# A feed-forward's first product by Strassen's algorithm, seven sub-products for eight

## The chip, the cores and the metric

The kernel runs on one core of a Trainium2 chip, in one launch. The metric is the device time of the whole program in microseconds; where several runs are compared, it is their median. The engines are TensorE (PE in the profile; its weight loads stand apart as PEld), VectorE (DVE), ScalarE (ACT), GpSimd (POOL) and SyncE (SP), which issues the DMAs. Each takes its instructions in the order in which they were queued, and they wait for each other by semaphores.

## The reference

The program is one inference step of a trunk of two layers over 640 tokens: 512 latent tokens and 128 context tokens, each of 1024 features. A layer is a feed-forward, a group of mixers and a second feed-forward, each on a normalised and modulated input and each added back through a gate:

```
x += gate1 * 0.5 * SwiGLU_1(mod(norm(x)))
x += gate2 * W_out [MLA | SWA-GQA+sink | bi-GatedDeltaNet](mod(norm(x)))
x += gate3 * 0.5 * SwiGLU_2(mod(norm(x)))

def swiglu(h, w1, w2):
    gate, up = jnp.split(h @ w1, 2, axis=-1)
    return (jax.nn.silu(gate) * up) @ w2
```

The inner width of a feed-forward is 2816, so `w1` is 1024 x 5632 and `w2` is 2816 x 1024. The shifts, scales and gates come from `silu(cond) @ w_ada + b_ada` (adaLN), with one condition for the latent tokens and one for the context tokens. All of it is in float32. The change touches the four feed-forwards, the adaLN work that is done inside them, and the end of each stage.

## The kernel before, in words

Activations are kept transposed: features on the 128 partitions, the 640 tokens along the row, in 8 tiles `x[0]` to `x[7]`. For precision every factor of a large product is split in two float32r parts, `hi` (a rounded copy, made by ScalarE) and `lo` (the rest, source minus `hi`, made by VectorE): `split`, which calls L67 and L70. A product is then three matmuls, hi x hi, lo x hi and hi x lo. `weight` loads a weight tile by a DMA on SP's queue and splits it in pieces of 128x512; `linear` (L104) runs the products of one 128-column weight block with all 640 tokens in two halves of 320 columns (`HALVES`), each in a PSUM bank of its own. A weight block of the first product is 8 feature tiles x 3 x 2 halves, 48 matmuls.

A feed-forward (`ffn`) starts with `modnorm`, which scales, shifts and splits the input (L169 to L171). Then it works in two halves of the inner width. In each half it goes over 11 column blocks `j`: the gate's 128 columns, SiLU on ScalarE (L229), the up-projection's 128 columns, the multiplication on VectorE (L232), and the split of the result in a pair of `mid` tiles. After the 11 blocks come the 8 output tiles `n` of the second product, each with 11 x 3 x 2 matmuls and an addition to `x` through the gate (`residual`, `addgate`, L188). The statistics of the next normalisation (`rstd`, `spread`) are computed at the last output tile.

The adaLN values that are needed later are computed in between: `fill` inserts one whole job of `adaln` behind a column block or an output tile. A job loads 8 tiles of 128x512 and multiplies each by the two conditions and accumulates (the first tile on ScalarE, L267; 7 x 2 steps on VectorE, L269), splits the two sums (ScalarE, and GpSimd at L273), sums over the partitions with 4 small matmuls (L275) and transposes the result with 4 more (L280).

The instructions are put on the engines' queues by a planner before the run: it follows the order of the program where it can, takes a later instruction when the earlier ones of that engine aren't ready by its own cost model, and lets an instruction wait for a buffer of its tag. `bufs` gives how many buffers a tag has: 3 for raw weight tiles, 4 for `whi` and for `wlo`, 22 for `mid`, 6 PSUM banks for products.

Two other lines serve in what follows as examples of operations beside each other: the rotary embedding in the mixer (`rope`, L307 and L309 on GpSimd, L308 on VectorE) and the convolution there (L395).

Of the kernel before, what the change touches and what calls it, by code (L numbers as in the profile page):

```python
# [6 lines left out]
F32 = mybir.dt.float32  # L7
# [14 lines left out]
NJ = DFF // P  # L22
EPS = 1e-6
# [18 lines left out]
class Net:  # L42
# [26 lines left out]
    def lo(self, dst, src, hi):  # L69
        self.nc.vector.tensor_tensor(dst, src, hi.bitcast(F32), ALU.subtract)  # L70

# [5 lines left out]
    def split(self, src, hi, lo):  # L77
        self.hi(hi, src)
        self.lo(lo, src, hi)

    def weight(self, src, kt, m):
        raw = self.wraw.tile([P, kt, m], F32, tag="wraw", name=self.nm("wr"))
        self.nc.sync.dma_start(raw, src)
        step = 512 // m
        out = []
        for k in range(0, kt, step):
            n = min(step, kt - k)
            hi, lo = (self.wsp.tile([P, n, m], F32R, tag=t, name=self.nm(t)) for t in ("whi", "wlo"))
            self.split(raw[:, k:k + n], hi, lo)
            out += [(hi[:, i, :], lo[:, i, :]) for i in range(n)]  # L90
        return out
# [35 lines left out]
    def rstd(self, pool, kind="G", windows=(0, 128, 256, 384, 512), last=True):  # L127

        nc = self.nc
        nb = len(windows)  # L130
        ps = self.pt(kind)
        r0, r = (pool.tile([P, nb], F32, tag="rs", name=self.nm("rs"), bufs=2) for _ in range(2))
        for i, t in enumerate(self.sq):
            for b, c in enumerate(windows):
                self.lastmm = nc.tensor.matmul(ps[:, 2 * b:2 * b + 2], lhsT=t[:, c:c + P], rhs=self.ones[:, :2],
                                               start=(i == 0 and b == 0), stop=(i == 1 and b == nb - 1))
# [56 lines left out]
    def residual(self, k, w, rhs, G, squares):  # L193


        if not squares:
            return self.addgate(k, self.linear(w, rhs), G)
        sq = self.xp.tile([P, T], F32, tag="sq", name=self.nm("sq"), bufs=3)
        if k < KD - 1:
            i = self.addgate(k, self.linear(w, rhs), G, sq)  # L200
            self.addsquare(sq)
            return i
        self.addsquare(sq)
        pool = _Bufs(self.const, dict(rs=4))
        ps = self.linear(w, rhs, cols=HALVES[:1])
        self.addgate(k, ps, G, sq, 0)
# [4 lines left out]
        ps += self.linear(w, rhs, cols=HALVES[1:], after={(5, 0): m, (10, 0): self.lastmm})  # L211
        i = self.addgate(k, ps, G, sq, 1)
        self.r = [row, self.rstd(pool, "G", WINDOWS[1])]
        return i


    def ffn(self, w1, w2, A, B, G):
        nc = self.nc
        with self.pool("ffn") as fp, self.banks(L=6, G=2):
            self.adap = fp  # L220
            h = self.modnorm_in(fp, A, B)
            for half in range(2):
                js = range(half * NJ // 2, (half + 1) * NJ // 2)
                mid = []
                for j in js:
                    pg = self.linear(self.weight(w1[j], KD, P), h)
                    sg = fp.tile([P, T], F32, tag="sg", name=self.nm("sg"), bufs=2)
                    for p, (c0, cw) in zip(pg, HALVES):
                        i1 = nc.scalar.activation(sg[:, c0:c0 + cw], p[:, :cw], AF.Silu)  # L229
                    pu = self.linear(self.weight(w1[NJ + j], KD, P), h)  # L230
                    for p, (c0, cw) in zip(pu, HALVES):
                        i0 = nc.vector.tensor_tensor(sg[:, c0:c0 + cw], p[:, :cw], sg[:, c0:c0 + cw], ALU.mult)  # L232
                    hi = fp.tile([P, T], F32R, tag="mid", name=self.nm("mh"), bufs=22)
                    lo = fp.tile([P, T], F32R, tag="mid", name=self.nm("ml"), bufs=22)
                    self.split(sg, hi, lo)
                    mid.append((hi, lo))
                    if j - js[0] in (3,5,7,9):
                        self.fill(i0, i1)
                for n in range(KD):
                    i0 = self.residual(n, self.weight(w2[half, n, :, :8], 8, P) + self.weight(w2[half, n, :, 8:], 3, P), mid, G, half == 1)  # L240
                    if n in (0,2,4):
                        self.fill(i0, i1)
# [5 lines left out]
    def adaln(self, l, i, start=False):  # L248
# [4 lines left out]
        ps = self.pt("G")  # L253
        if start:
            for q in range(KD):
# [3 lines left out]
        else:  # L259
            acc = [ap.tile([P, 512], F32, tag=t, name=self.nm(t), bufs=2) for t in ("ada0", "ada1")]  # L260
            for q in range(KD):
                raw = ap.tile([P, 512], F32, tag="adaw", name=self.nm("adaw"), bufs=4)
                nc.sync.dma_start(raw, a['wada'][l, i, q])
                for g in range(2):
# [3 lines left out]
                    else:  # L268
                        nc.vector.scalar_tensor_tensor(acc[g], raw, c, acc[g], ALU.mult, ALU.add)  # L269
            for g in range(2):  # L270
                hi, lo = (ap.tile([P, 512], F32R, tag=t, name=self.nm(t), bufs=1) for t in ("adah", "adal"))
                self.hi(hi, acc[g])
                nc.gpsimd.tensor_tensor(lo, acc[g], hi.bitcast(F32), ALU.subtract)  # L273
                for n, x in enumerate((hi, lo)):
                    nc.tensor.matmul(ps[:2, :], lhsT=self.sel[:, g, :], rhs=x, start=(g + n == 0), stop=(g + n == 2))  # L275
        row = ap.tile([2, 512], F32, tag="adarow", name=self.nm("adarow"), bufs=1)
# [16 lines left out]
    def fill(self, *after):  # L293

        if len(self.jobs) > self.hold:
            with self.tc.issue_after(after[0].ins), self.tc.issue_after(after[1].ins):
                self.adaln(*self.jobs.pop(0))
# [17 lines left out]
    def mixer(self, l, A, B, G):  # L315
# [180 lines left out]
        with self.pool("wo") as wp:  # L496
# [19 lines left out]
            with self.banks(L=6, G=2):  # L516
                order = (8, 9, 10, 11, 4, 5, 6, 7, 0, 1, 2, 3)
                for n in range(KD):
                    w = self.weight(a['wo'][l, n, :, 8:], 4, P) + self.weight(a['wo'][l, n, :, :8], 8, P)
                    w = w[:4] + w[8:] + w[4:8]  # L520
                    self.residual(n, w, [o[i] for i in order], G, True)
# [540 lines left out]
    def body(self):  # L1062
# [6 lines left out]
        self.wraw, self.wsp = E("wraw", 3), E("wsp", 4)  # L1069
# [28 lines left out]
        self.jobs = []  # L1098
        with self.pool("ada") as self.adap, self.banks(G=2, N=1):
            for i in (0, 2, 1, 3):  # L1100
                self.adaln(0, i, start=True)
# [32 lines left out]
        self.jobs, self.hold = [(0, i) for i in range(4, 18)], 0  # L1134
        for l in range(L):
            self.hold = 0
# [3 lines left out]
            if l + 1 < L:  # L1140
                self.jobs = [(l + 1, i) for i in range(18)]
                self.hold = 11
            self.ffn(a['w1b'][l], a['w2b'][l], *mods(2))
        with self.pool("fin") as fp, self.banks(G=4):
# [65 lines left out]
def _layout(x):  # L1210
# [9 lines left out]
    for s, n in (('a', 'ffn1'), ('b', 'ffn2')):  # L1220
        out['w1' + s] = tiles(x[n + '_w1'], KD, P)
        out['w2' + s] = C(x[n + '_w2'].reshape(L, 2, NJ // 2, P, KD, P).transpose(0, 1, 4, 3, 2, 5))
# [51 lines left out]
```

## Time and profile before

| | us |
|---|---|
| median of 3 runs | 3321.58 |
| lowest and highest | 3320.39, 3327.34 |
| the profiled execution's own time | 3325.07 |
| span of the profile, first to last instruction | 3323.3 |

The profile shows one execution. Busy times are sums over instructions, as shares of the span; TensorE's matmuls are pipelined, so that the duration of one is longer than the distance from one to the next. A group of rows is named by source line, engine, operation and tiles, "out<-in". The mean granted clock of TensorE is 0.987 of its full rate.

### The profile page before, as it was taken

The numbers are of one execution on the slowest core, as the hardware profiler recorded it, in microseconds if no ns is written. First come the engines' busy times: TensorE is split into PE (matmuls) and PEld (weight loads), VectorE is DVE, ScalarE is ACT, GpSimd is POOL, SyncE is SP. The second block draws the span as 40 slices with busy tenths as digits, with TensorE's granted clock in tenths as the row PEclk, the third lists the DMA queues.
The fourth block names the chain that finished last, engine by engine and source line by source line (L and its number), as shares of the span: only waits on it lengthen the run. The fifth ranks groups of instructions, "written<-read, shape, count | busy, mean of one in ns | idle before, by whom it ended". The sixth has DMA issues, their size and how long they took to land.

```text
span 3323.3 us, 56733 instructions
## 1 busy us (share of the span) xinstructions
PE 3241.5 (98%) x22036; PEld 3129.5 (94%) x22036; DVE 1886.3 (57%) x4357; ACT 1384.8 (42%) x3041; POOL 452.2 (14%) x480
## 2 busy tenths in 40 slices
PE   8999999999998999999999999999999989999998
PEld 5999999999887999999999999999998879999998
DVE  4564577686885355643346735477878653433333
ACT  3332334554676433322233323255466763321222
POOL 0000011222343100100000100012114340000000
PEclk9999999999999999999999999999999999999999
DMA  6443453322714224522224534333235242222222
GB/s 212 128 149 116 134 164 127 97 76 91 201 54 138 84 86 133 155 94 72 69 92 143 156 99 139 98 103 110 72 121 152 75 138 74 69 73 74 83 65 76
DMA packets 180190, 364.78 MB, mean 110 GB/s; under 512 B 28112, under 2 KB 68176, under 8 KB 179920
## 3 DMA queue, kind: packets, MB, share of 16 engines
q1 hardware_dynamic: 179920, 361.15, 35.2%
q8 instruction: 173, 2.83, 0.4%
q14 instruction: 97, 0.79, 0.1%
HBM read 315.03 MB, written 46.04 MB: 109 GB/s over the span
## 4 chain that ended last, share of the span: by engine, by line
PE 87%; DVE 6%; ACT 3%; DMA 2%; issue 2%; SPq 0%; POOL 0%; POOLq 0%; DVEq 0%; ACTq 0%
PE psL L104 72%; PE psT L942 3%; PE psG L703 3%; PE psS L1036 2%; PE psT L931 1%; PE psG L275 1%; PE psS L742 1%; DMA of<-do 1%; PE psS L745 1%; ACT pr L910 1%; PE psS L981 1%; DVE hf L169 1%; DMA adaw<-in_wada_dram 0%; DVE wlo L70 0%; PE psS L776 0%
## 5 line engine op out<-in xcount | busy, mean ns | idle before, releaser
L70 DVE TENSOR_TENSOR wlo<-wr,whi 128x512 fp32r<-128x512 f32 (+2 forms) x726 | 494.2, 682 | 709.5 <-ACT whi L67 708.0
L67 ACT ACTIVATE whi<-wr 128x512 fp32r<-128x512 f32 (+2 forms) x726 | 446.2, 616 | 876.2 <-PE psL L104 614.9
L104 PE MATMUL psL<-hb,whi 128*128 128x320 f32 x1968 | 523.8, 313 | 0.7 <-DVE hb L171 0.5
L104 PE MATMUL psL<-hc,whi 128*128 128x320 f32 x1952 | 521.0, 314 | 0.0
L104 PE MATMUL psL<-ha,whi 128*128 128x320 f32 x1856 | 492.3, 312 | 5.0 <-DVE ha L171 3.7
L104 PE MATMUL psL<-hd,whi 128*128 128x320 f32 (+1 forms) x1856 | 486.3, 310 | 1.9 <-DVE hd L171 1.9
L104 PE MATMUL psL<-mh,wlo 128*128 128x320 f32 x1408 | 434.2, 309 | 0.0
L104 PE MATMUL psL<-ml,whi 128*128 128x320 f32 x1408 | 434.0, 309 | 0.0
L104 PE MATMUL psL<-mh,whi 128*128 128x320 f32 x1408 | 432.9, 310 | 0.0
L104 PEld LDWEIGHTS psL<-hb,whi 128*128 128x128 f32 x1968 | 351.9, 189 | 2.6 <-DVE hb L171 1.2
L104 PEld LDWEIGHTS psL<-hc,whi 128*128 128x128 f32 x1952 | 349.4, 189 | 0.8
L104 PEld LDWEIGHTS psL<-ha,whi 128*128 128x128 f32 x1856 | 329.8, 188 | 8.6 <-DVE ha L171 5.7
L104 PEld LDWEIGHTS psL<-hd,whi 128*128 128x128 f32 (+1 forms) x1856 | 328.9, 188 | 5.2 <-DVE hd L171 3.1
L269 DVE SCALAR_TENSOR_TENSOR ada<-adaw,cs,ada 128x512 f32<-128x512 f32 x448 | 313.7, 743 | 0.0
L104 PE MATMUL psL<-hb,wlo 128*128 128x320 f32 (+1 forms) x984 | 307.3, 312 | 0.0
L104 PE MATMUL psL<-hc,wlo 128*128 128x320 f32 (+1 forms) x976 | 305.6, 313 | 0.0
L104 PE MATMUL psL<-hd,wlo 128*128 128x320 f32 (+1 forms) x928 | 287.7, 310 | 0.0
L104 PE MATMUL psL<-ha,wlo 128*128 128x320 f32 (+1 forms) x928 | 287.5, 311 | 0.0
L104 PEld LDWEIGHTS psL<-ml,whi 128*128 128x128 f32 x1408 | 264.0, 188 | 2.8
L104 PEld LDWEIGHTS psL<-mh,whi 128*128 128x128 f32 x1408 | 263.5, 188 | 3.0
L104 PEld LDWEIGHTS psL<-mh,wlo 128*128 128x128 f32 x1408 | 264.1, 188 | 2.0
L273 POOL TENSOR_TENSOR adal<-ada,adah 128x512 fp32r<-128x512 f32 x64 | 89.8, 1404 | 1041.7 <-ACT adah L67 823.3
(299 smaller groups left out, 5612.1 us busy)
## 6 DMA issues: line engine op xcount, KB each, us to landing
adaw<-in_wada_dram SPq DMA_DIRECT2D x288, 256.0 KB, 2.9
wr<-in_w1a_dram SPq DMA_DIRECT2D x88, 512.0 KB, 3.7
wr<-in_w1b_dram SPq DMA_DIRECT2D x88, 512.0 KB, 3.5
wr<-in_win_dram SPq DMA_DIRECT2D x54, 512.0 KB, 3.5
wr<-in_w2a_dram SPq DMA_DIRECT2D x32, 512.0 KB, 4.0
wr<-in_w2b_dram SPq DMA_DIRECT2D x32, 512.0 KB, 3.5
wr<-in_wo_dram SPq DMA_DIRECT2D x16, 512.0 KB, 3.6
dqn<-hd SPq DMA_DIRECT2D x24, 320.0 KB, 3.1
```

What stands on the lines that cost most here:

```text
L67: self.nc.scalar.activation(dst, src, AF.Copy)
L70: self.nc.vector.tensor_tensor(dst, src, hi.bitcast(F32), ALU.subtract)
L104: i = nc.tensor.matmul(p[:m, :cw], lhsT=w[:, :m], rhs=r[:, c0:c0 + cw], start=(k == 0 and n == 0), stop=(k == kt - 1 and n == 2))
L169: nc.vector.scalar_tensor_tensor(t[:, c0:c0 + n], self.x[k][:, s], A[:, k, g:g + 1], r[j][:, c0:c0 + n], ALU.mult, ALU.mult)
L269: nc.vector.scalar_tensor_tensor(acc[g], raw, c, acc[g], ALU.mult, ALU.add)
L273: nc.gpsimd.tensor_tensor(lo, acc[g], hi.bitcast(F32), ALU.subtract)
L275: nc.tensor.matmul(ps[:2, :], lhsT=self.sel[:, g, :], rhs=x, start=(g + n == 0), stop=(g + n == 2))
L703: nc.tensor.matmul(p[:, s], lhsT=lhs[:, s], rhs=rhs[:, s], start=True, stop=True)
L742: nc.tensor.matmul(p1[:, :P], lhsT=qw[:, u, c, 64 * d:64 * d + P], rhs=S, start=True, stop=True)
L745: nc.tensor.matmul(p2[:, :P], lhsT=KD_[d][c][:, us], rhs=UU[d][:, us], start=True, stop=True)
L942: nc.tensor.matmul(po[:, oc:oc + w], lhsT=vv[:, vb, :], rhs=hl[ti][:, s0:s0 + w], start=(n == 0), stop=(n == len(place) - 1))
L1036: nc.tensor.matmul(p[:, j, :w], lhsT=x[:96, qc], rhs=y[:96, k0 + j * w:k0 + j * w + w], start=(i == 0), stop=(i == 2))
```

## The change

The gate's and the up-projection's column block `j` are taken together as a 256-row by 1024 matrix in 2 x 2 parts, `a11` and `a12` for the gate's first and second 512 features, `a21` and `a22` for the up-projection's. The input is taken in 2 x 2 parts too, by feature halves and by column halves of 320 tokens. From the third block on, `block` computes the product by Strassen's algorithm in Winograd's form: four sums of weights `s1` to `s4` on GpSimd for each block, four sums of activations `t1` to `t4` once for each feed-forward (`sums` in `combos`, on GpSimd, split by ScalarE and VectorE), seven products of 4 feature tiles x 3 matmuls, and additions of the results out of PSUM on VectorE. Two of the seven `lo` parts (`a12`, `a22`) are made by GpSimd. The first two blocks are multiplied as before. `combos` takes the place of `modnorm` in the feed-forwards; GpSimd adds the shift to the unsplit input, which the sums need, and these unsplit tiles lie in the `mid` buffers, of which there are 12.

The inner width is worked in four passes of 5, 5, 6 and 6 blocks, each followed by its share of the second product, so that an output tile is added to `x` four times. The adaLN jobs become generators, cut in five portions; `fill` runs two behind each block and one behind every second output tile. Twelve jobs are done in the first feed-forward, ten in the second, ten in the third, none in the fourth (14, 7, 11 and 0 before). Raw weight tiles are loaded in pieces of 128x512, with 6 buffers. The last two output tiles of a feed-forward are closed together (`closing`): first halves of both, the statistics, then the second halves.

```diff
+PASSES = (5, 5, 6, 6)
...
-    def split(self, src, hi, lo):
+    def split(self, src, hi, lo, gpsimd=False):
         self.hi(hi, src)
-        self.lo(lo, src, hi)
+        (self.nc.gpsimd if gpsimd else self.nc.vector).tensor_tensor(lo, src, hi.bitcast(F32), ALU.subtract)
...
+    def parts(self, raw, gpsimd=False):
+
+        hi, lo = (self.wsp.tile([P, *raw.shape[1:]], F32R, tag=t, name=self.nm(t)) for t in ("whi", "wlo"))
+        self.split(raw, hi, lo, gpsimd)
+        return [(hi[:, i, :], lo[:, i, :]) for i in range(raw.shape[1])]
...
     def weight(self, src, kt, m):
...
         step = 512 // m
...
+        return [w for k in range(0, kt, step) for w in self.parts(self.load(src[:, k:min(k + step, kt)]))]
...
+            first = [self.weight(w, KD, P) for w in (w1[0], w1[NJ])]
+            h, sums = self.combos(fp, A, B)
+            j = 0
+            for size in PASSES:
                 mid = []
...
+                for _ in range(size):
+                    sg = low("sg", 2)
+                    if j < 2:
+                        for n, w in enumerate((w1[j], w1[NJ + j])):
+                            w = first[n] if j == 0 else self.weight(w, KD, P)
+                            for c in range(2):
+                                p = self.pt("L")[:, :320]
+                                self.products(p, w, h[c])
...
+                        if j == 0:
+                            t = sums()
+                    else:
+                        i0, i1 = self.block(fp, w1[j], w1[NJ + j], h, t, sg)
+                    m = [fp.tile([P, T], F32R, tag="mid", name=self.nm("mid"), bufs=12) for _ in range(2)]
+                    self.split(sg.rearrange("p a b -> p (a b)"), *m)
+                    mid.append(m)
+                    j += 1
+                    self.fill(2, i0, i1)
+                w = lambda n: self.weight(w2[n, :, j - size:j], size, P)
+                for n in range(KD - 2 if j == NJ else KD):
+                    i0 = self.residual(n, w(n), mid, G, j == NJ)
+                    if n % 2 == 0:
+                        self.fill(1, i0, i1)
+            self.closing((6, 7), [w(6), w(7)], mid, G)
...
+                        nc.gpsimd.tensor_scalar(t[:, c], t[:, c], B[:, k, g:g + 1], None, ALU.add)
...
+            for k in range(4):
+                t = lambda: fp.tile([P, 320], F32, tag="tsum", name=self.nm("ts"), bufs=4)
...
+                sub(t1, b12, b11)
+                keep(0, k, t1)
+                sub(t2, b22, t1)
+                keep(1, k, t2)
+                sub(t3, b22, b12)
+                keep(2, k, t3)
+                sub(t4, b21, t2)
+                keep(3, k, t4)
...
+    def block(self, fp, a1, a2, h, T_, sg):
...
+        ws = lambda: fp.tile([P, 4, P], F32, tag="ws", name=self.nm("ws"), bufs=4)
+        a11, a21, a12, a22 = (self.load(x) for x in (a1[:, :4], a2[:, :4], a1[:, 4:], a2[:, 4:]))
...
+        pt(s1, a21, a22, ALU.add)
+        nc.scalar.activation(u, product(a11, False, b11), AF.Copy)
+        pt(s2, s1, a11, ALU.subtract)
+        add(sg[:, 0], u, product(a12, True, b21))
+        nc.scalar.activation(sg[:, 0], sg[:, 0], AF.Silu)
+        pt(s3, a11, a21, ALU.subtract)
+        p5 = product(s1, False, t1)
+        pt(s4, a12, s2, ALU.subtract)
+        add(u, u, product(s2, False, t2))
+        add(sg[:, 1], u, p5)
+        add(u, u, product(s3, False, t3))
+        add(w, u, p5)
+        add(sg[:, 1], sg[:, 1], product(s4, False, b22))
+        i1 = nc.scalar.activation(sg[:, 1], sg[:, 1], AF.Silu)
+        add(u, u, product(a22, True, t4))
+        tt(sg[:, 0], sg[:, 0], u, ALU.mult)
+        i0 = tt(sg[:, 1], sg[:, 1], w, ALU.mult)
+        return i0, i1
...
-                raw = ap.tile([P, 512], F32, tag="adaw", name=self.nm("adaw"), bufs=4)
+                raw = ap.tile([P, 512], F32, tag="adaw", name=self.nm("adaw"), bufs=3)
...
+                if q % 2:
+                    yield
...
+    def fill(self, n, *after):
+
+        with self.tc.issue_after(after[0].ins), self.tc.issue_after(after[1].ins):
+            for _ in range(n):
+                next(self.job, None)
...
-        self.wraw, self.wsp = E("wraw", 3), E("wsp", 4)
+        self.wraw, self.wsp = E("wraw", 6), E("wsp", 4)
```

## Rows read from the trace of the kernel before

**Rows 1.** The page: busy time, share and instructions of each engine.

```profile
PE 3241.5 (98%) x22036; PEld 3129.5 (94%) x22036; DVE 1886.3 (57%) x4357; ACT 1384.8 (42%) x3041; POOL 452.2 (14%) x480
```

**Rows 2.** The page: the chain that ended last, by line.

```profile
PE psL L104 72%; PE psT L942 3%; PE psG L703 3%; PE psS L1036 2%; PE psT L931 1%; PE psG L275 1%; PE psS L742 1%; DMA of<-do 1%; PE psS L745 1%; ACT pr L910 1%; PE psS L981 1%; DVE hf L169 1%; DMA adaw<-in_wada_dram 0%; DVE wlo L70 0%; PE psS L776 0%
```

**Rows 3.** Windows, the four feed-forwards: stretch, length, busy us by engine, clock, DMA.

```profile
48.00:539.00 491.00, 489.88 (x3304) 479.65 (x3302) 295.69 (x521) 170.95 (x311) 40.91 (x29) 1.00 0.43 132
...
1208.00:1683.00 475.00, 474.51 (x3228) 469.79 (x3226) 226.35 (x397) 148.94 (x271) 20.62 (x15) 1.00 0.33 102
1689.00:2172.00 483.00, 483.00 (x3271) 475.86 (x3270) 264.82 (x465) 159.93 (x291) 30.85 (x23) 1.00 0.39 121
...
2842.00:3310.00 468.00, 467.86 (x3186) 467.78 (x3185) 163.76 (x292) 127.53 (x234) 0.85 (x1) 1.00 0.22 69
```

**Rows 4.** The chain in order of time, first and fourth feed-forward: start, length.

```profile
135.34 0.34 PE psG L280 x4
135.68 18.38 PE psL L104 x124
154.05 0.23 PE psG L275
...
165.29 18.38 PE psL L104 x124
...
2842.41 460.49 PE psL L104 x3130
```

**Rows 5.** Groups of instructions, shapes apart, fourth feed-forward: busy us, mean ns.

```profile
L67 ACT ACTIVATE whi<-wr 128x512 fp32r<-128x512 f32 x116 | 72.9, 630 | 197.3 <-PE psL L104 121.7 <-issue 74.4 <-ACT hd L170 1.0
...
L232 DVE TENSOR_TENSOR sg<-psL,sg 128x320 f32<-128x320 f32 x44 | 21.6, 491 | 50.9 <-PE psL L104 46.8 <-ACT sg L229 4.0
...
L188 DVE SCALAR_TENSOR_TENSOR x<-psL,G,x 128x320 f32<-128x320 f32 x16 | 8.8, 550 | 50.7 <-PE psL L104 50.7
```

**Rows 6.** VectorE's timeline in the first feed-forward: start us, us.

```profile
109.48 0.68 DVE L70 TENSOR_TENSOR wlo<-wr,whi 128x512 fp32r<-128x512 f32 x1
110.08 0.74 DVE L269 SCALAR_TENSOR_TENSOR ada<-adaw,cs,ada 128x512 f32<-128x512 f32 x1
110.74 0.82 DVE L70 TENSOR_TENSOR ml<-sg,mh 128x640 fp32r<-128x640 f32 x1
111.48 2.73 DVE L269 SCALAR_TENSOR_TENSOR ada<-adaw,cs,ada 128x512 f32<-128x512 f32 x4
...
118.65 0.48 DVE L232 TENSOR_TENSOR sg<-psL,sg 128x320 f32<-128x320 f32 x1
119.05 1.40 DVE L269 SCALAR_TENSOR_TENSOR ada<-adaw,cs,ada 128x512 f32<-128x512 f32 x2
```

**Rows 7.** Single lines, all instructions: duration ns min/median/max, first and last start.

```profile
L273 POOL TENSOR_TENSOR adal<-ada,adah x64: 1293/1295/2414, 121.3 to 2095.7; 128x512 fp32r<-128x512 f32 x64
L308 DVE TENSOR_TENSOR stg<-stg,rope x16: 678/1758/1784, 564.9 to 2515.6; 128x512 f32<-128x512 f32 x14, 32x512 f32<-32x512 f32 x2
L395 DVE SCALAR_TENSOR_TENSOR cv<-pad,small,cv x96: 840/879/1676, 564.0 to 2388.3; 128x644 f32<-128x644 f32 x96
```

**Rows 8.** Timeline of VectorE and GpSimd in a mixer: start us, us.

```profile
2281.37 0.67 DVE L70 TENSOR_TENSOR wlo<-wr,whi 128x512 fp32r<-128x512 f32 x1
2281.62 1.55 POOL L307 TENSOR_TENSOR rt<-rt,rope 128x512 f32<-128x512 f32 x1 [13.71 <-DVE rt L306]
2281.96 1.76 DVE L308 TENSOR_TENSOR stg<-stg,rope 128x512 f32<-128x512 f32 x1
...
2320.83 1.29 POOL L668 TENSOR_TENSOR A<-QK,dec 128x512 f32<-128x512 f32 x1
2320.87 0.87 DVE L665 SCALAR_TENSOR_TENSOR U<-psG,sc,dec 128x128 f32<-128x128 f32 x3
2321.65 1.15 DVE L70 TENSOR_TENSOR cv<-stg,pad 128x640 fp32r<-128x640 f32 x1
```

**Rows 9.** GpSimd's timeline in a mixer: start us, us.

```profile
2365.17 0.20 POOL L762 MEMSET st<- 128x128 f32 x1
```

More of the change, by code (lines that the diff above doesn't have):

```diff
@@ L218, in ffn @@
         nc = self.nc
+        tt = nc.vector.tensor_tensor
         with self.pool("ffn") as fp, self.banks(L=6, G=2):
             self.adap = fp
-            h = self.modnorm_in(fp, A, B)
-            for half in range(2):
-                js = range(half * NJ // 2, (half + 1) * NJ // 2)
-                mid = []
[L225 to L242, printed above, removed]
@@ new lines, in block, with product @@
+    def block(self, fp, a1, a2, h, T_, sg):
+        nc = self.nc
+        tt, pt = nc.vector.tensor_tensor, nc.gpsimd.tensor_tensor
+        t1, t2, t3, t4 = T_
+        b11, b21, b22 = h[0][:4], h[0][4:], h[1][4:]
+        ws = lambda: fp.tile([P, 4, P], F32, tag="ws", name=self.nm("ws"), bufs=4)
+        a11, a21, a12, a22 = (self.load(x) for x in (a1[:, :4], a2[:, :4], a1[:, 4:], a2[:, 4:]))
+        s1, s2, s3, s4 = ws(), ws(), ws(), ws()
+        u, w = (fp.tile([P, 320], F32, tag="tsum", name=self.nm("tsum"), bufs=4) for _ in range(2))
+        def product(w, gpsimd, rhs):
+            p = self.pt("L")[:, :320]
+            self.products(p, self.parts(w, gpsimd), rhs)
+            return p
+        add = lambda d, x, y: tt(d, x, y, ALU.add)
+        pt(s1, a21, a22, ALU.add)
[16 more added lines that the diff above has]
+        return i0, i1
@@ L291, in adaln, with work @@
             nc.vector.tensor_scalar(self.G[l][j][:, h, :], dst, (0.5, 1.0, 0.5)[j], None, ALU.mult)
[L293 to L297, printed above, removed]
+    def fill(self, n, *after):
+        with self.tc.issue_after(after[0].ins), self.tc.issue_after(after[1].ins):
+            for _ in range(n):
+                next(self.job, None)
+    def work(self, jobs):
+        for l, i in jobs:
+            yield from self.adaln(l, i)
+            yield
     def rope(self, pool, z, np_, kind, mask):
@@ L1133, in body @@
             nc.vector.tensor_scalar(self.nsink[:, l * 8:l * 8 + 8], self.sm(l, 'sink'), -1.0, None, ALU.mult)
-        self.jobs, self.hold = [(0, i) for i in range(4, 18)], 0
+        jobs = [(l, i) for l in range(L) for i in range(18)]
+        self.job = self.work(jobs[4:16])
         for l in range(L):
-            self.hold = 0
             mods = lambda j: (self.A[l][j], self.mods[l][:, 3 * j], self.G[l][j])
@@ L1139, in body @@
             self.mixer(l, *mods(1))
-            if l + 1 < L:
-                self.jobs = [(l + 1, i) for i in range(18)]
-                self.hold = 11
+            self.job = self.work(jobs[16:26] if l == 0 else ())
             self.ffn(a['w1b'][l], a['w2b'][l], *mods(2))
+            self.job = self.work(jobs[26:])
         with self.pool("fin") as fp, self.banks(G=4):
```

120 lines of the change are left out of this document (87 added, 33 removed).

## The prediction

> **What bounds the kernel now.** I read the busy times first: TensorE is busy for 98% of the span, VectorE for 57%, ScalarE for 42%, GpSimd for 14% [rows 1]. A busy share of matmuls alone proves little, so the chain of waits came next: 72% of it is one line, the weight products of L104 [rows 2]. Then the four feed-forwards, called F1 to F4 in order of time, by windows [rows 3]: 491, 475, 483 and 468 us, with TensorE's granted clock at 1.00 (the 2.4 GHz level) and TensorE busy all through, VectorE for 164 to 296 us of each, GpSimd for 1 to 41 us. Last, the pace. F4's chain has 3130 products in 460.49 us, 0.147 us each [rows 4]. In F1 two column blocks of 96 products and one adaLN job repeat every 29.61 us (135.68 to 165.29); 192 x 0.147 = 28.2 us are products, and the job's small matmuls are 4 x 0.23 + 0.34 = 1.26 us [rows 4]. So nothing but TensorE sets the pace: a product left out saves 0.147 us, as long as the other engines keep up.
>
> The Trainium skill (TensorE: Matmul & The Clock Gate, "Back-to-back issue gap") gives an isolated warm gap of N / 2.4 + 2.5 ns, 136 ns for 320 columns. The row's 147 ns differs; by the page the saving below would be 130 us, by the row 141, and the row decides.
>
> **What is removed.** A block has 7 x 4 x 3 = 84 products for 96; 20 of 22 blocks in each of 4 feed-forwards: 960 fewer, 141.1 us. A block falls from 96 x 0.147 = 14.11 us to 12.35.
>
> **What is added, and where.** Per block, by prices from one start to the next in VectorE's timeline [rows 6]: a lo half of 128x512 0.60 us, an adaLN step 0.66, a lo half of 128x640 0.74, an operation on 320 PSUM columns 0.40 (0.49 as a duration [rows 5]). GpSimd's 128x512 subtraction takes 1.295 [rows 7].
> - VectorE with both inputs in SBUF (D): 5 lo halves 3.00, the mid's lo half 0.74, two multiplications of 320 columns, not in the trace, taken as 0.40 each: 4.54 us.
> - VectorE reading one PSUM input (F): 7 additions of 0.40: 2.80 us.
> - GpSimd (P): four sums of weights and two lo halves, 6 x 1.295 = 7.77 us.
> - ScalarE gets 3 more hi halves; it is busy 128 to 171 us of a feed-forward [rows 3], so these 3 x 20 x 0.63 us [rows 5] stay hidden.
>
> Each engine alone fits into 12.35 us. But P and D don't run together. L308, two SBUF inputs, takes 678 ns at least and 1758 at the median [rows 7]: at 2281.96 it starts while GpSimd runs L307 from 2281.62 for 1.55, ends at 2283.72, 0.55 after GpSimd; and GpSimd's own 1.55 holds 0.26 of waiting for the lo half before [rows 8]. L395, the form of the adaLN step (two SBUF inputs and a scalar), goes from 879 to 1676 ns [rows 7]. An operation with a PSUM input isn't stopped: three L665 run from 2320.87 in 0.87 us beside a GpSimd operation that starts at 2320.83, and the lo half behind them ends only 0.68 us after it [rows 8]. So P and D add up, 12.31 us a block, F at best lies under P, and all in a row is 15.11.
>
> The Trainium skill (Perfetto Trace Analysis, "Optimizing Scalar/DVE Operations") says that these two engines share an SBUF port, so that moving work between them might not help. That speaks against the two lo halves put on GpSimd: by it they bring nothing, and at the rows' prices they ask the pair for 2 x (1.295 - 0.60) = 1.4 us more per block.
>
> An adaLN job asks the pair for 14 x 0.66 + 2 x 1.295 = 11.83 us. It is now cut into 5 portions of 2.37 us, two behind each block and one behind every second output tile of the second product: 60 portions in F1, 50 in F2 and in F3, none in F4.
>
> How much of F is uncovered? In a block with portions GpSimd has 6.8 operations, each of which waits for about one D (0.60): 6.8 x 1.9 = 12.9 of some 17.7 us in which it holds the pair or stands ready to, 73%, so 27% of F, 0.75 us, is added: 13.06 us. Without portions 6 x 1.9 = 11.4 of 12.7, so 0.35 is added: 12.66 us. The bounds are 0 and 2.80.
>
> How much is done ahead, while TensorE works on the second product? The four sums of the next block (4 buffers) and the splits of its first two sub-products as the four split buffers, which the second weights share, come free: 4 x 1.295 + 0.60 + 1.295 = 7.1 us. The bounds are 0 and all of the pair's spare time. There is room: such a stage is 8 x 5 x 6 x 0.147 = 35.3 us of TensorE, and the pair needs 8 x 0.60 plus small lo halves (6.4) and some six portions (14). Its 24 gate additions, 0.55 us the longest [rows 5], are F. Over a feed-forward their number doubles, 48 more, under 27 us in all, which lies under the same stages.
>
> Now the stretches of blocks before each second product. The last block's two portions run behind it, so a stretch of 5 has 8 portions and one of 6 has 10.
> - First (2 plain blocks, 3 of Strassen): 8 lo halves and two of the mid 6.3; the 16 sums of activations, on 320 columns (0.81 + 0.40) x 16 = 19.4; 3 x 13.06; 8 x 2.37: 83.9 us. Nothing is ahead. Before: 5 x 14.11 + 2.0 for jobs = 72.6. +11.3.
> - Five: 65.3 + 19.0 - 7.1 = 77.2 against 72.6: +4.6.
> - Six: 78.4 + 23.7 - 7.1 = 95.0 against 87.2: +7.8. In F2 and F3 the last has six portions: 85.5 against 86.2, -0.7.
>
> F1: 11.3 + 4.6 + 7.8 + 7.8 = +31.5. F2 and F3: 23.0 each, +46. In F4 TensorE is again slower than the pair (first 63.7 against 65.3, five 56.2 against 61.75, six 68.9 against 74.1): -5.3 - 8.8 - 10.6 - 10.6 = -35.3. Together +42.
>
> **The start and the end.** At the start GpSimd adds the shift to each tile in place; eight of these come between VectorE's instructions of the first half, whose two-step chain TensorE waits for. A GpSimd operation with one input of 320 columns is not in the trace: below 0.50 (a 128x128 memset is 0.20 [rows 9]) to 0.81 (1.295 x 320/512); I take 0.62, 5 us a feed-forward, +20. A new wait is there too: the 12 mid buffers hold the normalised input until its sums are made, so the first block's mid, VectorE's queue behind it and the third block's scratch wait for GpSimd; that lies in the +11.3. The closing of two output tiles together lets the statistics run beside 24 products or so: 0 to 2 us each, -4. The loads are halved in size and doubled in number at the same bytes; the DMA engines are busy 22 to 43% [rows 3], and six buffers hold them: nothing. If a raw tile were late, GpSimd's sum would be the next late thing.
>
> Sum: +58 us on the execution's own 3325.07 is 3383. That execution lies 3.5 us above the median of the runs shown, so **3380 us**, slower by 1.7%. The forecast's own range is 3330 to 3455, from an F share of 0.4 with 10 us ahead to one of 1.3 with 3 us ahead.
>
> **Rivals.**
> - *Levelled* (faster). Where GpSimd, VectorE and TensorE are decoupled by more than I think, the pair's need spreads over the whole feed-forward: in F1 20 x 12.31 + 6.3 + 19.4 + 12 x 11.83 + 28 (second weights) + 25 (start, squares) = 467 against 491 now, and F2 to F4 are TensorE's, -35 each: -130 + 16, 3207 us. It begins where the work ahead of each of the nine later stretches grows by 58 / 9, from 7.1 to about 13.5 us. For it: VectorE's idle time in F1 is 195 us. Against it: four split buffers. Halfway is 3295.
> - *No lock in these forms* (faster): then TensorE paces all blocks: -141 + 16, 3197 us. Against it are the 1758 and the 1676 ns.
> - *A chain through the queues* (slower still): VectorE's queue waits at an F for its product, that product for a lo half of GpSimd, which waits for VectorE. Then no F is covered and nothing is ahead: 60 blocks x 2.05, nine stretches x 7.1, and F4 at +17 for -35, so +239 more, 3620 us. For it: both engines' queues are in order, and 7 sub-products alternate between them.
> - *No change*: the terms happen to cancel, 3315 to 3328.
> - That the products aren't saved is excluded by the count.
>
> **How the numbers follow.** This kernel's runs spread over 0.2%, 6.6 us, which is what can be told from no change. Chances: forecast 0.45; chain, in part or whole, above 3455, 0.15; no change 0.07; levelled 0.28; no lock 0.05. So slower 0.60, same 0.07, faster 0.33. The range 3235 to 3490 leaves out the no-lock case and the lowest of the levelled one (0.10) and the upper half of the chain (0.10).
>
> **What would show it.** In F1 to F3 a Strassen block with portions should take 15 to 18 us, in F4 12.4 to 13; the lo halves of L70's successor should show many durations near 1.8 us, and GpSimd 1.6 to 1.9 for 1.295; TensorE should wait for wlo, with its granted clock still at 1.00. TensorE without gaps in F1 to F3 would make the prediction wrong, towards the levelled case; gaps in F4 too, towards the chain.

## The result, and the profile after

The changed kernel takes 3429.32 us (median of 4 runs, 3425.34 to 3430.40) against 3323.07 for the kernel before: a ratio of 1.0316, 95% interval 1.0298 to 1.0334. It is slower by 106 us, where 58 were forecast: the forecast's direction, its own range (3330 to 3455) and its mechanism held, and its size was little more than half.

The page of the changed kernel: busy time by engine, and the chain that ended last, by engine.

```profile
PE 3193.9 (93%) x21124; PEld 3029.2 (88%) x21124; DVE 2620.6 (76%) x5313; ACT 1586.6 (46%) x3489; POOL 1369.7 (40%) x1120
...
PE 61%; DVE 22%; issue 6%; ACT 4%; POOL 4%; DMA 3%; SPq 0%; DVEq 0%; POOLq 0%; ACTq 0%
```

Against [rows 1], TensorE is no longer busy all through, though it has fewer instructions; VectorE and GpSimd have some 730 and 920 us more, and VectorE is now 22% of the chain. The products themselves were saved. The question is in which stretches they were lost again, so windows come next. First two stretches of five and six Strassen blocks in the first feed-forward (F1), with adaLN portions, then the same in the fourth (F4), without; columns as in [rows 3].

```profile
185.00:262.00 77.00, 68.52 (x436) 64.09 (x435) 73.15 (x97) 34.77 (x64) 49.65 (x31) 0.98 0.35 105
299.00:392.00 93.00, 82.52 (x524) 77.25 (x523) 89.21 (x119) 40.10 (x74) 56.29 (x37) 0.98 0.37 112
...
3081.00:3142.00 61.00, 61.00 (x418) 60.93 (x417) 51.13 (x75) 29.60 (x55) 35.62 (x25) 1.00 0.24 75
3178.00:3252.00 74.00, 74.00 (x503) 73.46 (x502) 62.53 (x91) 35.67 (x66) 44.27 (x31) 1.00 0.25 79
```

Behind the length of each window come TensorE (PE), its weight loads and VectorE (DVE). In F1 VectorE is busy, time in which an instruction is held up by GpSimd included, for 73 of 77 and 89 of 93 us, and TensorE has gaps; in F4 TensorE has none and VectorE has room. From the start of the first product to that of the last, stretches of five measured 77.3, 78.3, 77.3 and 61.5 us in F1 to F4, the first stretches of six 92.6, 93.6, 92.8 and 74.3, F1's second 91.9. Forecast were 77.2 and 61.75, 95.0 and 74.1.

What a blocked instruction looks like: VectorE and GpSimd in F2's stretch of five (start us, us).

```profile
1403.48 1.78 DVE L77 TENSOR_TENSOR wlo<-ws,whi 128x512 fp32r<-128x512 f32 x1
1405.18 0.47 DVE L353 TENSOR_TENSOR tsum<-tsum,psL 128x320 f32<-128x320 f32 x1
1405.39 1.30 POOL L361 TENSOR_TENSOR ws<-wr,ws 128x512 f32<-128x512 f32 x1 [0.68 <-POOL ws L359]
1405.68 0.49 DVE L353 TENSOR_TENSOR sg<-tsum,psL 128x320 f32<-128x320 f32 x1
1406.09 1.15 DVE L77 TENSOR_TENSOR wlo<-wr,whi 128x512 fp32r<-128x512 f32 x1
1406.65 1.72 POOL L77 TENSOR_TENSOR adah<-ada,adah 128x512 fp32r<-128x512 f32 x1
```

The additions out of PSUM (L353) keep their 0.47 to 0.49 us beside GpSimd's L361. The lo half at 1406.09 starts while GpSimd's L361 runs, which ends at 1406.69, and ends 0.55 us after it: 1.15 us in all. GpSimd's next, from 1406.65, starts while that lo half runs and takes 1.72 for 1.295. By groups, shapes apart (mean ns behind the comma): first the kernel before, the adaLN step over the whole run and the lo half in F4, then the changed kernel in that stretch.

```profile
L269 DVE SCALAR_TENSOR_TENSOR ada<-adaw,cs,ada 128x512 f32<-128x512 f32 x448 | 313.7, 743 | 0.0
L70 DVE TENSOR_TENSOR wlo<-wr,whi 128x512 fp32r<-128x512 f32 x116 | 80.1, 692 | 176.0 <-ACT whi L67 175.6
```

```profile
L399 DVE SCALAR_TENSOR_TENSOR ada<-adaw,cs,ada 128x512 f32<-128x512 f32 x22 | 23.9, 1100 | 2.1 <-ACT ada L397 1.9
L77 DVE TENSOR_TENSOR wlo<-ws,whi 128x512 fp32r<-128x512 f32 x20 | 20.0, 1008 | 0.2 <-ACT whi L68 0.2
L353 DVE TENSOR_TENSOR tsum<-tsum,psL 128x320 f32<-128x320 f32 x19 | 9.1, 481 | 1.1 <-PE psL L100 0.7
```

The adaLN step went from 743 ns to 1100, the lo half from 692 to 1008, while the operation with a PSUM input took 481, and 483 in F4 of idle_memsets (below), where GpSimd does not read beside it.

Where the forecast of Strassen's own cost was shortest is the first stretch, F4's above all. GpSimd's timeline at F4's start:

```profile
2960.71 1.77 POOL L311 TENSOR_SCALAR mid<-mid,mod 128x320 f32<-128x320 f32 x1 [7.86 <-DVE rs L148]
2962.45 1.01 POOL L149 TENSOR_TENSOR rs<-rs,mhalf 128x3 f32<-128x3 f32 x1
2963.46 13.29 POOL L311 TENSOR_SCALAR mid<-mid,mod 128x320 f32<-128x320 f32 x14
2976.73 0.90 POOL L323 TENSOR_TENSOR ts<-mid,mid 128x320 f32<-128x320 f32 x1
2977.61 7.84 POOL L311 TENSOR_SCALAR mid<-mid,mod 128x128 f32<-128x128 f32 x9
...
3014.77 1.11 POOL L323 TENSOR_TENSOR ts<-mid,mid 128x320 f32<-128x320 f32 x1
3015.84 1.12 POOL L323 TENSOR_TENSOR ts<-mid,ts 128x320 f32<-128x320 f32 x1
3019.79 1.29 POOL L77 TENSOR_TENSOR wlo<-wr,whi 128x512 fp32r<-128x512 f32 x1 [2.83 <-DMA wr<-in_w1b_dram]
```

From 2960.7 to 3017 GpSimd has hardly a gap: 24 shifts for 22.9 us, 16 sums of activations, and the first blocks' own operations between them. The chain of waits follows it from 2986 to 3014 (18% of the window 2986 to 3046 in the sums L323, 17% in the weight sums), and TensorE takes 54.9 us for three blocks' 252 products. The operations in this queue are lengthened too, the weight sums to as much as 1.88 us for 1.295, so both the queue's length and VectorE beside it count here.

By ends of stages the 105.3 us of span are: F1 +37.9, the first mixer +6.4, F2 +42.3, F3 +32.4, the second mixer +0.2, F4 -13.9.

### The profile page after: what moved, and what is told of

The parts are those of the page before. It is cut to its first block, busy times and chain, and to the rows that moved or that the text cites. A ratio compares the mean times of both kernels' runs of the same rounds, so it can differ in the third digit from the quotient of the medians.

```text
span 3428.6 us, 58576 instructions
## 1 busy us (share of the span) xinstructions
PE 3193.9 (93%) x21124; PEld 3029.2 (88%) x21124; DVE 2620.6 (76%) x5313; ACT 1586.6 (46%) x3489; POOL 1369.7 (40%) x1120
## 4 chain that ended last, share of the span: by engine, by line
PE 61%; DVE 22%; issue 6%; ACT 4%; POOL 4%; DMA 3%; SPq 0%; DVEq 0%; POOLq 0%; ACTq 0%
PE psL L113 31%; PE psL L100 15%; DVE ada L399 6%; DVE wlo L77 5%; PE psT L1082 3%; PE psG L843 3%; DVE mid L77 2%; DVE tsum L353 2%; PE psS L1176 1%; PE psT L1071 1%; DVE sg L353 1%; DVE sg L369 1%; DMA of<-do 1%; PE psS L882 1%; PE psS L885 1%
## 5 line engine op out<-in xcount | busy, mean ns | idle before, releaser
L68 ACT ACTIVATE whi<-wr 128x512 fp32r<-128x512 f32 (+3 forms) x710 | 400.6, 574 | 527.7 <-PE psL L113 340.8
L113 PE MATMUL psL<-mid,whi 128*128 128x320 f32 x2816 | 627.5, 309 | 0.0
L77 DVE TENSOR_TENSOR wlo<-wr,whi 128x512 fp32r<-128x512 f32 (+3 forms) x550 | 378.6, 696 | 185.9 <-ACT whi L68 183.3
L100 PE MATMUL psL<-hx,whi 128*128 128x320 f32 x1920 | 492.6, 318 | 18.2 <-DVE hx L77 15.1
L113 PEld LDWEIGHTS psL<-mid,whi 128*128 128x128 f32 x2816 | 472.9, 188 | 3.7 <-ACT whi L68 0.4
L113 PE MATMUL psL<-mid,wlo 128*128 128x320 f32 x1408 | 433.0, 310 | 1.4 <-DVE wlo L77 1.2
L100 PEld LDWEIGHTS psL<-hx,whi 128*128 128x128 f32 x1920 | 344.1, 193 | 27.6 <-DVE hx L77 21.9
L77 DVE TENSOR_TENSOR wlo<-ws,whi 128x512 fp32r<-128x512 f32 x320 | 321.1, 1008 | 12.1 <-ACT whi L68 11.3
L100 PE MATMUL psL<-hb,whi 128*128 128x320 f32 x768 | 190.1, 314 | 15.5 <-DVE tsum L353 15.5
L100 PE MATMUL psL<-hc,whi 128*128 128x320 f32 x768 | 190.6, 317 | 0.4 <-ACT whi L68 0.4
L353 DVE TENSOR_TENSOR tsum<-tsum,psL 128x320 f32<-128x320 f32 x320 | 153.8, 480 | 37.7 <-PE psL L100 31.8
```

Of the source, the lines that this page charges most:

```text
L68: self.nc.scalar.activation(dst, src, AF.Copy)
L77: (self.nc.gpsimd if gpsimd else self.nc.vector).tensor_tensor(lo, src, hi.bitcast(F32), ALU.subtract)
L100: self.nc.tensor.matmul(p, lhsT=w, rhs=r, start=(first and k + n == 0), stop=(last and k == kt - 1 and n == 2))
L113: i = nc.tensor.matmul(p[:m, :cw], lhsT=w[:, :m], rhs=r[:, c0:c0 + cw], start=(k == 0 and n == 0), stop=(k == kt - 1 and n == 2))
L353: add = lambda d, x, y: tt(d, x, y, ALU.add)
```

## The experiments

The theory: a VectorE instruction with two SBUF inputs and a GpSimd instruction that reads SBUF take turns, and their sum paces the blocks. The rivals: VectorE's own load; waits in a circle between queues, with GpSimd's results late; for the first stretch, GpSimd's queue. Times are medians, each beside runs of the kernel before on the same chip (3326 to 3327 us).

**lo_on_vector.**

```diff
-        add(sg[:, 0], u, product(a12, True, b21))
+        add(sg[:, 0], u, product(a12, False, b21))
...
-        add(u, u, product(a22, True, t4))
+        add(u, u, product(a22, False, t4))
```

> The lo halves of a12 and a22 are made by VectorE again, all else as in the changed kernel. Theory (GpSimd and VectorE instructions with two SBUF inputs add up): each block asks the pair for 2 x (1.295 - 0.60) = 1.4 us less. A stretch of five with adaLN portions falls from 77.3 to about 71 us, of six from 93 to about 85, the fourth feed-forward's stay at 61.5 and 74.3 (TensorE): about 25 us in each of the first three, in all 3355 us (3340 to 3375). Rival 1 (VectorE's own load sets the pace, GpSimd runs beside it): 1.2 us more for each of 60 blocks, 3500 us. Rival 2 (waits in a circle between the queues set it): no change beyond 15 us.

Measured: 3401.63 us, ratio to before 1.0227 (1.0212 to 1.0243), 28 us below the changed kernel. More instructions for VectorE, and faster: VectorE's own load isn't the pace. The gain is 28 us for 75 expected, between the theory and Rival 2; stretches of six fell to 85 to 89 us, of five only to 73 to 74 us for 409 of their 420 products. Part of the shortfall lies in the expectation: by the prediction's own rule, GpSimd's four sums a block cover less of F than its six operations did, some 1.3 us instead of 0.75 stay uncovered, and a gain of 0.85 us a block was due, not 1.4 (an estimate from the prediction's terms).

**no_weight_sums.**

```diff
-        s1, s2, s3, s4 = ws(), ws(), ws(), ws()
+        s1, s2, s3, s4 = a21, a11, a12, a21
...
-        pt(s1, a21, a22, ALU.add)
...
-        pt(s2, s1, a11, ALU.subtract)
...
-        pt(s3, a11, a21, ALU.subtract)
...
-        pt(s4, a12, s2, ALU.subtract)
```

(The tiles a21 and a22 are loaded into the four `ws` buffers, so that the prefetch is as deep.)

> The four sums of weights of each block are left out: raw weight tiles stand in for s1 to s4, so GpSimd has 2 operations a block for 6, VectorE, ScalarE and TensorE as many as before. Theory: the pair needs 7.1 us a block, less than TensorE's 12.35, so TensorE sets the pace: with portions a stretch of five takes about 64 us for 77.3, of six 77 for 93; 3260 us (3240 to 3290). Rival 1 (VectorE's own load): no change, 3430. Rival 2 (waits in a circle): VectorE's waits for GpSimd's sums go too, so it can fall as well, but blocks stay above 14 us.

Measured, in one run: 3260.89 us, at the theory's 3260. Its windows of five and six in F1 and of five in F4:

```profile
175.00:236.00 61.00, 60.52 (x409) 58.83 (x408) 55.02 (x89) 33.20 (x61) 19.52 (x13) 1.00 0.40 125
275.00:351.00 76.00, 76.00 (x516) 74.70 (x515) 71.61 (x118) 40.91 (x75) 23.12 (x15) 1.00 0.45 133
2913.00:2973.00 60.00, 60.00 (x411) 60.00 (x410) 40.05 (x74) 29.16 (x54) 11.67 (x9) 1.00 0.28 84
```

TensorE has no gaps worth the name, and a stretch of six takes 76.7 us for 92.6, 12.8 a block, where Rival 2 wanted more than 14, with VectorE's instructions as many as in the changed kernel. So the pace came from GpSimd's sums; by the port or by their late results isn't told apart here (below).

**shift_on_scalar.**

```diff
-                        nc.gpsimd.tensor_scalar(t[:, c], t[:, c], B[:, k, g:g + 1], None, ALU.add)
+                        nc.scalar.activation(t[:, c], t[:, c], AF.Identity, bias=B[:, k, g:g + 1])
```

> The shift that GpSimd adds to the unsplit input (24 operations a feed-forward, 0.95 us each in the profile) is added by ScalarE. Theory (GpSimd's queue, 56 us long without a gap at the start of the fourth feed-forward, sets the first stretch): the queue gets 23 us shorter, and each first stretch 8 to 13 us: 3390 us (3375 to 3400). Rival (the first stretch is set by the sum of both engines only, or by VectorE's two-step chain): under 15 us in all, 3415 to 3430.

Measured: 3401.32 us, 28 us below the changed kernel, for 39 expected. The blocks of the first stretch in F4 take 45.9 us for 54.9; the stretches of five and six stay (76.8 to 77.3 and 92.8 to 93.6 in F1 to F3). The shifts were on the path, 5 to 12 us a feed-forward; the rival, under 15 us in all, falls.

**portions_moved.**

```diff
-                    self.fill(2, i0, i1)
+                    self.fill(2 if j <= 5 else 1, i0, i1)
...
-                    if n % 2 == 0:
-                        self.fill(1, i0, i1)
+                    self.fill(2 if j == 5 and n % 2 == 0 else 1, i0, i1)
```

> The adaLN portions are moved: two behind each of the first five blocks as before, then one behind each block and one behind every output tile (two behind every second one in the first pass). Theory: a stretch of five loses 4 x 2.37 us and falls from 77.3 to 68, of six from 93 to 81, last six of the second and third feed-forward to 76; the second product's stages have room for them and grow by under 2 us each: 3345 us (3325 to 3370). Rival (waits in a circle inside a block): the blocks keep 15 us and more, and the total falls by less than 40.

Measured: 3408.83 us, ratio 1.0247 (1.0232 to 1.0263), 20 us below for 84 expected. By its numbers this is the rival's case: less than 40 us, and blocks of more than 15 us in the stretch of five, which got longer, 82.5 us. The second product's stage and the stretch behind it in F1:

```profile
148.00:185.00 37.00, 36.42 (x245) 35.26 (x244) 34.49 (x68) 12.34 (x25) 10.73 (x7) 1.00 0.57 166
186.00:268.00 82.00, 69.75 (x440) 64.47 (x439) 81.21 (x109) 35.35 (x67) 49.85 (x31) 0.98 0.39 115
```

The trace shows another reason than waits in a circle. VectorE is busy for 34.5 of 37 us in that stage (31.0 in the changed kernel) and does 20 adaLN steps there, where the changed kernel does 16; the rest of the 12 portions goes into the next stretch, which has 28 steps for 22, though it was laid out with four portions fewer, and VectorE is busy for 81.2 of its 82 us. My expectation had not counted VectorE's gate additions and work ahead in that stage.

**all_blocks_plain.** Every block takes the branch `if j < 2`; no sums, no unsplit input.

> The changed kernel with every block multiplied plainly (96 products, no sums of either kind, no unsplit input); passes, portions, loads and closing stay. Theory: TensorE sets the pace again and the rest of the change costs nothing: 3315 to 3330 us. Rival (four passes, finer portions and doubled output additions cost time by themselves): above 3340.

Measured: 3344.62 us, ratio 1.0054 (1.0039 to 1.0069). Its stretches of six take 87.3 us in F1 to F3, which is TensorE's 84.7 us and the small matmuls of two adaLN jobs, and the rest of the change costs 18 us by itself, as the rival said: F2 is 8 us longer than before (it has three more adaLN jobs), the mixers 4 and 2, F4 3, F3 2, F1 none. Why, beyond the jobs and the closing (below), isn't settled. Of the 106 us, then, some 88 are Strassen's own.

**weights_on_vector.** lo_on_vector, and the weight sums on VectorE:

```diff
-        tt, pt = nc.vector.tensor_tensor, nc.gpsimd.tensor_tensor
+        tt, pt = nc.vector.tensor_tensor, nc.vector.tensor_tensor
```

> The two lo halves and the four sums of weights are made by VectorE, so GpSimd has no part in a block. VectorE then needs 4.54 + 6 x 0.60 + 2.80 = 10.9 us a block alone. Theory: the pair is relieved of 6 x 0.7 us a block: a stretch of five with portions takes 5 x 10.9 + 8 x 2.37 - 3.6 done ahead = 70 us for 77, of six 86 for 93; 3370 us (3350 to 3390), below lo_on_vector. Rival (VectorE's own instructions, not the port, were the load): 2.4 us more per block than lo_on_vector, 3450 us or above.

Measured: 3308.25 us, ratio 0.9944 (0.9929 to 0.9959): 121 us below the changed kernel, although VectorE has six more instructions in each of 80 blocks, and faster than the kernel before. Against lo_on_vector it is 93 us less, where the rival wanted 50 more. It is also below the range expected: the first stretches, for which I had counted nothing, fell by 6 to 8 us each, and those of five and six with portions went to 67 to 70 and 79 to 82 us, for 70 and 86. VectorE has no time left in them: in F2's first stretch of six it is busy for all of the 79 us, GpSimd for 6.6, while F4's, without portions, leaves VectorE room (F4 first).

```profile
3058.00:3131.00 73.00, 73.00 (x500) 73.00 (x499) 65.86 (x120) 36.37 (x66) 0.00 (x0) 1.00 0.25 76
1439.00:1518.00 79.00, 76.41 (x504) 74.51 (x504) 79.00 (x145) 41.01 (x74) 6.59 (x4) 0.98 0.40 122
```

**weights_and_shift.**

> weights_on_vector and shift_on_scalar together. Theory: the two act on different stretches, so their gains add up: 28 us below weights_on_vector, about 3342 us (3320 to 3365). Rival (both relieve the same thing): less than 12 us below weights_on_vector.

Measured: 3290.23 us, ratio 0.9891 (0.9875 to 0.9907), 18 us below weights_on_vector, between the theory's 28 and the rival's 12. Most of the gain adds up; that GpSimd's queue at the start had become shorter already, with the weight sums gone from it, would explain the rest, but no run shows it.

**levelled.** weights_and_shift, the adaLN split on VectorE, and

```diff
-                    self.fill(2, i0, i1)
+                    self.fill(2 if j <= 5 else 1, i0, i1)
...
-                    if n % 2 == 0:
-                        self.fill(1, i0, i1)
+                    self.fill(2 if j == NJ and n < 3 else 1, i0, i1)
```

> As weights_and_shift, with the adaLN split on VectorE too and the portions laid so that no stretch needs more of VectorE than TensorE's time: two behind each of the first five blocks, one behind each later block, one behind every output tile (two behind the first three of the last pass). Theory: a stretch of five needs 54.7 + 4 x 2.1 - 3.6 = 59.5 us of VectorE against 62.8 of TensorE, the second product's stage 15 + 8 x 2.1 + 3.6 = 35.4 against 36.3, so TensorE sets the pace in all but the first stretches: 3240 us (3215 to 3280), faster than the kernel before. Rival (queue order and buffers keep the engines from running beside each other whatever the sums): blocks with portions stay above 14 us and the total above 3300.

Measured: 3294.95 us, ratio 0.9910 (0.9893 to 0.9926), no better than weights_and_shift. F2 and F3 gained 2.6 us and lost 0.5; F1 lost 12, its last stage grew from 47.0 to 56.8 us under the portions laid there. Stretches of six stayed at 78 to 79 us, 4 above F4's 73.8. In the first one of F1, half of that is the small matmuls of two adaLN jobs, 1.26 us each. GpSimd does nothing in it, and VectorE is busy for 77.7 of 79 us (66.0 of 73 in F4), where the expectation wanted it to have room. So VectorE's own work is the likely cause of the other half; no run tests it.

**idle_reads and idle_memsets** tell the port from late results. Both are weights_on_vector with work for GpSimd whose results nobody in the feed-forward waits for, paced by one small operation that reads the block's result `w`:

```diff
+        z = self.bd[0]
+        nc.gpsimd.tensor_tensor(z[:32, :8], w[:32, :8], self.mhalf[:32], ALU.mult)
+        for _ in range(6):
+            nc.gpsimd.tensor_tensor(z, z, self.bd[2], ALU.mult)
```

and, for idle_memsets, in place of the last two lines:

```diff
+        for _ in range(18):
+            nc.gpsimd.memset(z, 0.0)
```

> weights_on_vector, and GpSimd multiplies two constant 128x512 tiles six times in each Strassen block, paced by one small operation that reads the block's result; nobody in the feed-forward waits for these. Theory (instructions of the two engines with SBUF inputs add up): the pair needs 8.1 + 7.8 = 15.9 us a block; the fourth feed-forward's stretch of five goes from 61.5 to about 80 us, of six from 74 to 97, the others by more: 3550 to 3780 us. Rival (what delayed the changed kernel was that VectorE, ScalarE and TensorE waited for GpSimd's late results, not the port): 3308 us, within 15.

> weights_on_vector, and GpSimd sets a constant 128x512 tile to zero 18 times in each Strassen block, paced in the same way; these read nothing. Theory (only GpSimd instructions that read SBUF add up with VectorE's): 3308 us, within 15. Rival (any GpSimd instruction on SBUF does): as idle_reads, in proportion to GpSimd's busy time.

Measured, one run each: 3682.33 and 3304.03 us. GpSimd's groups, idle_reads first:

```profile
L374 POOL TENSOR_TENSOR bd<-bd,bd 128x512 f32<-128x512 f32 x480 | 744.1, 1550 | 35.0
```

```profile
L374 POOL MEMSET bd<- 128x512 f32 x1440 | 759.7, 528 | 79.6
```

And F4's stretch of six, windows of idle_reads and of idle_memsets:

```profile
3386.00:3480.00 94.00, 77.20 (x502) 73.52 (x501) 91.85 (x119) 34.24 (x65) 47.72 (x35) 1.00 0.19 56
```

```profile
3053.00:3125.00 72.00, 72.00 (x493) 72.00 (x492) 65.21 (x119) 35.39 (x64) 49.12 (x97) 1.00 0.25 76
```

GpSimd's added work keeps it busy for about as long in both, 744 and 760 us in all, and GpSimd is busy for 48 and 49 us in the stretch. Reading two tiles, it costs 374 us and takes TensorE from no gaps to 77 of 94 us; only writing, it costs nothing. Nobody waits for a result in either, and the small read of `w` is in both. In idle_reads VectorE's two multiplications of 320 columns, both inputs in SBUF, took 1573 and 1571 ns on average, the additions out of PSUM 479; in idle_memsets the same multiplications took 484 (last line):

```profile
L353 DVE TENSOR_TENSOR tsum<-tsum,psL 128x320 f32<-128x320 f32 x23 | 11.0, 479 | 0.8 <-PE psL L100 0.3
L370 DVE TENSOR_TENSOR sg<-sg,tsum 128x320 f32<-128x320 f32 x5 | 7.9, 1573 | 0.0
L369 DVE TENSOR_TENSOR sg<-sg,tsum 128x320 f32<-128x320 f32 x5 | 7.9, 1571 | 0.0
...
L370 DVE TENSOR_TENSOR sg<-sg,tsum 128x320 f32<-128x320 f32 x5 | 2.4, 484 | 0.0
```

So GpSimd's reads alone, without a late result, cost as much as the theory says: F4's stretches of five and six went to 77.8 and 94.4 us, where about 80 and 97 were expected. How the 121 us of weights_on_vector divide between this and late results isn't measured. In the changed kernel late results look like the small part: in the chain of waits, GpSimd's own operations have 11% of F1's stretch of five and 5% of its first of six, VectorE's 45 and 68%.

The Trainium skill (SBUF — State Buffer, "Who interferes with whom") states this rule: a VectorE instruction with two SBUF inputs contends with a GpSimd instruction that reads SBUF, not with one that only writes it. The two runs agree with it.

**one_preload.** weights_and_shift with one weight block ahead of the normalised input:

```diff
-            first = [self.weight(w, KD, P) for w in (w1[0], w1[NJ])]
+            first = [self.weight(w1[0], KD, P)]
```

> weights_and_shift, with one weight block (512 KB) loaded ahead of the normalised input for two. Theory (the second block's 512 KB lie ahead of TensorE's first product at the program's start, which came at 54.3 us for 47.6): 3284 us (3280 to 3288). Rival (the start waits for something else): 3290, within 3.

Measured: 3291.01 us, ratio 0.9890 (0.9873 to 0.9906): no change, the rival's case. The theory of the start falls. It also began from a misreading: 54.3 us is not the first product of the changed kernel but the start of its first longer run; the first comes at 48.7, for 47.6 before.

**one_tile_closing.** one_preload, with

```diff
-                for n in range(KD - 2 if j == NJ else KD):
+                for n in range(KD - 1 if j == NJ else KD):
...
-            self.closing((6, 7), [w(6), w(7)], mid, G)
+            self.closing((7,), [w(7)], mid, G)
```

> one_preload, with the last output tile of a feed-forward closed alone, as before the change. Theory (the closing of two tiles together costs, as the last stages of 45.7 us for 288 products say): 5 to 10 us below one_preload. Rival (it gains what it was costed at, 1 us each): 0 to 5 us above it.

Measured: 3283.95 us, ratio 0.9870 (0.9855 to 0.9885), 7 us below one_preload; the two intervals overlap a little, but F2, F3 and F4 each got shorter, by 2.8, 1.6 and 1.4 us. Closing two tiles together costs rather than gains. This is the fastest of the versions that make all the sums: 1.3% faster than the kernel before, 4.2% than the changed one.

## Why the prediction was right, and where its size was off

- *TensorE paced everything, and a product saved is 0.147 us.* Right: beside the plain blocks of all_blocks_plain, F4's stretches, where TensorE has no gaps, fell by 8.7 and 10.0 us, forecast 8.8 and 10.6.
- *VectorE and GpSimd take turns.* Right, and shown for VectorE's instructions with two SBUF inputs and GpSimd's that read: by the durations above, by weights_on_vector (more work on VectorE, 121 us less), and by idle_reads beside idle_memsets.
- *The sums for the stretches.* Five: 77.2 forecast, 77.3 to 78.3 measured. Six: 95.0 against 91.9 to 93.6. The last six of F2 and F3: 85.5 against 88.4 and 87.9. Two of the terms were guesses, 7.1 us done ahead and 0.75 us of F uncovered per block. GpSimd's timeline at the start of F1's stretch of five, at 185.16 us, shows somewhat less ahead:

```profile
179.21 1.30 POOL L354 TENSOR_TENSOR ws<-wr,wr 128x512 f32<-128x512 f32 x1 [18.79 <-DMA wr<-in_w1a_dram]
180.59 1.30 POOL L356 TENSOR_TENSOR ws<-ws,wr 128x512 f32<-128x512 f32 x1
181.85 1.75 POOL L359 TENSOR_TENSOR ws<-wr,wr 128x512 f32<-128x512 f32 x1
183.55 1.75 POOL L361 TENSOR_TENSOR ws<-wr,ws 128x512 f32<-128x512 f32 x1
185.26 1.74 POOL L77 TENSOR_TENSOR wlo<-wr,whi 128x512 fp32r<-128x512 f32 x1
```

The four sums are there and one lo half of VectorE (at 184.06), 5.8 us at the prediction's prices; GpSimd's lo half, counted too, starts behind 185.16. So the fives came out within about 1 us partly by errors that cancel, which is luck; the same bookkeeping overrated lo_on_vector by 47 us and portions_moved by 64. For portions_moved the step it lacked is VectorE's own time in the second product's stage.

- *The start and the first stretch*: the step that was mis-sized. "Eight of these come between VectorE's instructions of the first half" counted 8 shifts of 0.62 us. There are 24, at 22.9 us in F4, and they stand ahead of the sums on GpSimd's queue, which the chain of waits follows there. Beside the plain blocks of all_blocks_plain the first stretch, from its first product on, is 19.5, 19.6 and 16.9 us longer in F1 to F3, where 16.3 was forecast (11.3 + 5), but 11.8 longer in F4, where the forecast had -0.3. That is the largest miss in one stretch, 12 us; moving the shifts took 9.0 us off F4.
- *The rest of the change*: four passes, finer portions, doubled additions and halved loads were put at nothing, the closing at -4 us. all_blocks_plain, which keeps all of these, is 18 us slower than the kernel before. That is 22 of the 48 us by which the forecast fell short; the other 26 are Strassen's own, 62 forecast (42 for the stretches, 20 for the start) and 88 measured.
- *The closing*: -1 us each was forecast; undoing it gained 1.4 to 2.8 us in F2 to F4. Miss: some 3 us each.
- *Small ones*, parts of the above: F2 does three adaLN jobs more than before, F1 two less, which I spread evenly (3.8 and 2.5 us); the sixtieth portion of F1 falls behind its end, into the first mixer's 6.4 us (what it costs there wasn't measured). At the program's start the 24th product comes at 58.1 us for 54.6. VectorE now makes eight unsplit tiles before the first lo half, at 52.37, as the new buffers allow; it was at 47.79 before. That this order is the cause was only read off the timeline.

TensorE's clock has a small part in F4's first stretch. The mean granted clock is 0.90 from 2955 to 2990 and 0.85 from 2990 to 3046; there it stands at 0.50 of the full rate (the 1.2 GHz level) from 3000.1 to 3006.8 and from 3010.4 to 3020.5, after TensorE had begun to wait at about 2996. Until 3013.7 the chain of waits goes through GpSimd, not through TensorE. Then 28 products from 3015.21 take 6.78 us, 0.242 each for 0.147, so 2.7 us more (an estimate from this row), of the 11.8 us that this stretch is longer.

Not settled: why the rest of the change costs as much as 18 us, beyond the jobs and the closing; how much of the 121 us was late results; and what the clock costs in the first stretches of F1 to F3.

## What to carry to other kernels

Before work is put on an idle GpSimd, count what VectorE does with two SBUF inputs in the same stretch and add the two up: six operations of 1.295 us cost more there than six of 0.60 on the busier VectorE. An operation count that saves 12.5% of the products needs a ledger for every engine and every stage: F4's stretches gained 8.7 to 10 us each, while those with adaLN portions lost. That buffers limit what a stage with room can do for the next was argued in the prediction; no run varied them. And read a queue as a whole: the cheap operations at its head (24 shifts) delayed the ones that mattered.

## What the runs showed of the hardware

- A GpSimd memset of 128x512 took 528 ns and 1440 of them cost VectorE and TensorE nothing (3304.03 against 3308.25 us); 480 multiplications that read and write the same size, 744 us busy, cost 374 us.
- GpSimd's addition of a per-partition scalar to one input takes longer than a memset suggests: 600 ns was the shortest of 96, of 128 to 320 columns, and 23 of them took 21.1 us in F4's start (13.29 + 7.84), 0.92 us each, time in which VectorE held them up included.
- An instruction blocked in this way shows no wait in the profile (0.2 us of idle time before 20 lo halves); it shows as a longer duration (1008 ns on average for 692), so busy time rises and the waits look innocent.
